# Rotary embedding with interleaved pairs: one buffer of five rows, and neighbouring rows in one transfer

## The chip, the cores and the metric

The kernel runs on one core of one Trainium2 chip. The metric is the device time of one execution in microseconds; shown is the median of three runs with the lowest and the highest.

## The reference

`x` has 8 batch rows of 2048 positions, 16 heads and 64 values in float32 (8.39 MB per row). Neighbouring values of a head are a pair, and each pair is turned by an angle that depends on the position and on the pair's place in the head:

```python
x_pairs = x.reshape(batch, seq_len, num_heads, head_dim // 2, 2)
x1 = x_pairs[..., 0]
x2 = x_pairs[..., 1]
cos = cos[None, :, None, :].copy()
sin = sin[None, :, None, :].copy()
out1 = x1 * cos - x2 * sin
out2 = x1 * sin + x2 * cos
out = np.stack([out1, out2], axis=-1).reshape(batch, seq_len, num_heads, head_dim)
```

Every value is read once from HBM and written once to HBM, both in float32.

## The kernel before

The unit of work is a batch row. Its 2048 positions lie on 128 partitions, 16 neighbouring positions on each (`K = 16`), so a partition holds one run of 64 KB of float32 in HBM and 32 KB of bfloat16 on the chip. The conversion from float32 to bfloat16 and back is done by the transfers themselves, and all these are issued by GpSimd: one queue (q0 in the profile), worked off in the order of issue by 16 DMA engines, each of which carries 8 partitions. Five buffers of one row each hold rows 0 to 4; rows 5, 6 and 7 take the buffers of rows 0, 1 and 2 once these are stored.

`rotate` (L71) turns a row in its buffer, with three VectorE instructions: a product with the sine table into a work buffer (L84), a product with the cosine table in place (L85), and the sum of the two with the work buffer read in swapped pairs (L90). Both tables are made once (L103 to L108), with the signs in the sine table.

The order of the instructions on each engine is the order of the program (`manual_schedule`). The start:

- SyncE loads the first four positions of row 0 as float32 (L94), and ScalarE converts them (L102). This is the other queue, q1.
- GpSimd issues the other twelve positions of row 0 (L95), cosine and sine (L96, L97), rows 1 to 3 (L98, L99), and row 4 in two transfers (L100, `load_fine`): twelve positions, then four positions in packets of at most 8 KB (L63, L64).

Then the loop over rows (L110): rotate a row, issue its store (L69), and from row 1 on issue the load of the row four further on (L122), which waits until the buffer's earlier row has been stored. Store 0 is issued as soon as row 0 is rotated, and so stands in the queue behind all five rows' loads. Between store 0 and store 1 GpSimd copies one element of row 4's last position into `mark` (L117): GpSimd waits there until row 4 has landed, so that store 1 and all that follows is issued after that.

The end: GpSimd stores the first twelve positions of row 7 (L123). The last four go another way: ScalarE writes one element of row 6's buffer (L128), which has to wait until store 6 has landed, then converts the four positions into float32 (L129), and SyncE stores them (L130) beside the twelve.

Of the kernel before, what the change touches and what calls it, by code (L numbers as in the profile page):

```python
# [2 lines left out]

# [4 lines left out]


@with_exitstack  # L10
def kernel(
    ctx: ExitStack,
    tc: tile.TileContext,
    x: bass.AP,
    cos: bass.AP,
    sin: bass.AP,
    out: bass.AP,
):
    nc = tc.nc
    fp32 = mybir.dt.float32  # L20
    bf16 = mybir.dt.bfloat16
    mult = mybir.AluOpType.mult
    add = mybir.AluOpType.add

    B, S, H, D = x.shape
    P = 128
    K = S // P
    KP = 16
    D2 = D // 2
    HD = H * D  # L30
    NX = 5
    HEAD = 4
    TAIL = 4
    FINE = 4
    FINE_BYTES = 8192


    x_t = x.rearrange("b (p k) h d -> b p k (h d)", p=P, k=K)
    out_t = out.rearrange("b (p k) h d -> b p k (h d)", p=P, k=K)
    cos_t = cos.rearrange("(p k) c -> p (k c)", p=P, k=K)  # L40
    sin_t = sin.rearrange("(p k) c -> p (k c)", p=P, k=K)

    consts = ctx.enter_context(tc.tile_pool(name="consts", bufs=1))
    xpool = ctx.enter_context(tc.tile_pool(name="xpool", bufs=NX))
    stage = ctx.enter_context(tc.tile_pool(name="stage", bufs=1))

    cos_sb = consts.tile([P, K * D2], fp32)
    sin_sb = consts.tile([P, K * D2], fp32)
    c_tab = consts.tile([P, K, D], bf16)
    s_tab = consts.tile([P, K, D], bf16)  # L50

    mark = consts.tile([1, 1], bf16)
    tiles = {}

    def load(b, k0=0):
        if b not in tiles:
            tiles[b] = xpool.tile([P, K, HD], bf16, name="xt")
        nc.gpsimd.dma_start(out=tiles[b][:, k0:], in_=x_t[b, :, k0:])  # L58

    def load_fine(b):  # L60
        tiles[b] = xpool.tile([P, K, HD], bf16, name="xt")
        k0 = K - FINE
        nc.gpsimd.dma_start(out=tiles[b][:, :k0], in_=x_t[b, :, :k0])  # L63
        nc.gpsimd.dma_start(  # L64
            out=tiles[b][:, k0:], in_=x_t[b, :, k0:], max_dma_last_dim=FINE_BYTES
        )

    def store(b, k1=K):
        nc.gpsimd.dma_start(out=out_t[b, :, :k1], in_=tiles[b][:, :k1])  # L69

    def rotate(b, k0, k1):  # L71
        nk = k1 - k0
        xp = tiles[b][:, k0:k1]
        qt = stage.tile([P, KP, HD], bf16, name="qt", tag="work")

        def rows(a):
            return a.rearrange("p k (h e) -> p k h e", h=H, e=D)

        def tab(a):
            return dataclasses.replace(  # L80
                a, offset=a.offset + k0 * D, ap=[a.ap[0], [D, nk], [0, H], [1, D]]
            )

        nc.vector.tensor_tensor(out=rows(qt[:, :nk]), in0=rows(xp), in1=tab(s_tab), op=mult)  # L84
        nc.vector.tensor_tensor(out=rows(xp), in0=rows(xp), in1=tab(c_tab), op=mult)  # L85
        q_swap = dataclasses.replace(
            qt, offset=qt.offset + 1, ap=[qt.ap[0], [2, nk * HD // 2], [-1, 2]]
        )
        x3 = xp.rearrange("p k (a j) -> p (k a) j", j=2)
        nc.vector.tensor_tensor(out=x3, in0=x3, in1=q_swap, op=add)  # L90

    with tc.manual_schedule():
        head = stage.tile([P, TAIL, HD], fp32, name="st", tag="work")
        nc.sync.dma_start(out=head[:, :HEAD], in_=x_t[0, :, :HEAD])  # L94
        load(0, HEAD)  # L95
        nc.gpsimd.dma_start(out=cos_sb, in_=cos_t)  # L96
        nc.gpsimd.dma_start(out=sin_sb, in_=sin_t)  # L97
        for b in range(1, NX - 1):  # L98
            load(b)  # L99
        load_fine(NX - 1)  # L100

        nc.scalar.copy(out=tiles[0][:, :HEAD], in_=head[:, :HEAD])  # L102
        s2 = s_tab.rearrange("p k (i j) -> p (k i) j", j=2)  # L103
        nc.vector.tensor_copy(out=s2[:, :, 0], in_=sin_sb)  # L104
        nc.vector.tensor_scalar_mul(s2[:, :, 1], sin_sb, -1.0)  # L105
        nc.vector.tensor_copy(  # L106
            out=c_tab.rearrange("p k (i j) -> p (k i) j", j=2),
            in_=cos_sb.to_broadcast([P, K * D2, 2]),  # L108
        )
        for b in range(B):  # L110
            if b == 0:
                rotate(b, 0, HEAD)
                rotate(b, HEAD, KP)
            else:
                rotate(b, 0, KP)
            if b == 1:
                nc.gpsimd.tensor_copy(out=mark, in_=tiles[NX - 1][:1, K - 1, :1])  # L117
            if b < B - 1:
                store(b)

            if b >= 1 and b - 1 + NX < B:
                load(b - 1 + NX)  # L122
        store(B - 1, K - TAIL)  # L123

        tail = stage.tile([P, TAIL, HD], fp32, name="st", tag="work")
        nc.scalar.copy(out=tiles[B - 2][:1, 0, :1], in_=tiles[B - 1][:1, K - 1, :1])  # L128
        nc.scalar.copy(out=tail, in_=tiles[B - 1][:, K - TAIL :])  # L129
        nc.sync.dma_start(out=out_t[B - 1, :, K - TAIL :], in_=tail)  # L130


# [1 line left out]
_INS = ['x', 'cos', 'sin']  # L134
_OUTS = [((8, 2048, 16, 64), 'float32')]


# [23 lines left out]
```

## Time and profile before

| what | value |
|---|---|
| median of 3 runs (lowest to highest) | 317.47 us (317.16 to 317.57) |
| span of the profiled execution | 315.7 us |
| transfers issued by GpSimd, by SyncE | 19, 2 |
| VectorE idle for want of a row, before rows 5, 6 and 7 | 3.7, 12.4 and 12.6 us |
| last instruction's issue (SyncE's store of row 7's end) | 299.25 us, 15.6 us to landing |

The span is that of one execution under the profiler; what the device time has beyond it lies before the first and after the last instruction. "To landing" is the time from the start of a transfer's issue to the moment when all 16 DMA engines have reported it done; since transfers queue up, it holds the wait behind the earlier ones. The GB/s of a load count its bfloat16 side, half of what is read from HBM.

### The profile page before, as it was taken

How to read it: one execution, taken by the hardware profiler on the slowest of the kernel's cores; microseconds unless marked ns; L12 is line 12 of the kernel's file. 1: busy time of each engine (PE TensorE's matmuls, PEld its weight loads, DVE VectorE, ACT ScalarE, POOL GpSimd, SP SyncE). 2: the span in 40 equal slices, each digit the busy share in tenths (PEclk: the TensorE clock that was granted, in tenths of full speed). 3: DMA queues.
4: the chain of work that ended last, by engine and by line, in shares of the span. 5: the costliest groups of instructions: out<-in, count | busy, mean ns of one | idle time of the engine just before them, and what ended most of it. 6: DMA issues, size and time to landing. Idle time of an engine off the chain costs nothing.

```text
span 315.7 us, 127 instructions
## 1 busy us (share of the span) xinstructions
DVE 210.4 (67%) x30; ACT 8.6 (3%) x4; POOL 12.6 (4%) x24
## 2 busy tenths in 40 slices
DVE  0009999999999999999869960899508994000000
ACT  1030000000000000000000000000000000000400
POOL 6000000000000201010000100000000000000000
DMA  7999999999999999999999999999999999999997
GB/s 257 257 282 199 199 228 237 199 199 257 201 206 266 399 482 448 399 332 257 208 399 399 394 203 199 432 498 266 199 291 440 399 399 515 415 399 423 426 432 313
DMA packets 3025, 102.24 MB, mean 324 GB/s; under 512 B 337, under 2 KB 337, under 8 KB 721
## 3 DMA queue, kind: packets, MB, share of 16 engines
q0 software_dynamic: 2736, 98.04, 96.8%
q1 hardware_dynamic: 288, 4.19, 3.3%
q14 instruction: 1, 0.00, 0.0%
HBM read 67.63 MB, written 67.11 MB: 427 GB/s over the span
## 4 chain that ended last, share of the span: by engine, by line
another core or an unknown queue 88%; DMA 5%; ACT 1%; ACTq 1%; issue 0%
DMA st<-in_x_dram 5%; ACT xt L102 1%; ACTq L156 1%; ACT xt L128 0%; ACTq L128 0%
## 5 line engine op out<-in xcount | busy, mean ns | idle before, releaser
L84 DVE TENSOR_TENSOR qt<-xt,s_tab 128x16384 bf16<-128x16384 bf16 (+2 forms) x9 | 69.7, 7744 | 28.8 <-DMA xt<-in_x_dram 28.6
L85 DVE TENSOR_TENSOR xt<-xt,c_tab 128x16384 bf16<-128x16384 bf16 (+2 forms) x9 | 69.7, 7743 | 0.4
L90 DVE TENSOR_TENSOR xt<-xt,qt 128x16384 bf16<-128x16384 bf16 (+2 forms) x9 | 69.7, 7744 | 0.3
L104 DVE CAST s_tab<-sin_sb 128x512 bf16<-128x512 f32 x1 | 0.5, 453 | 23.9 <-DMA sin_sb<-in_sin_dram 23.9
L69 POOL DMA_DIRECT2D out_dram<-xt x8 | 4.3, 538 | 128.7 <-DVE xt L90 128.7
L128 ACT COPY xt<-xt 1x1 bf16<-1x1 bf16 x1 | 0.2, 192 | 276.6 <-DMA out_dram<-xt 276.6
L58 POOL DMA_DIRECT2D xt<-in_x_dram x7 | 3.9, 572 | 73.8 <-DMA out_dram<-xt 73.0
L102 ACT CAST xt<-st 128x4096 bf16<-128x4096 f32 x1 | 3.6, 3604 | 13.3 <-DMA st<-in_x_dram 13.3
L117 POOL COPY mark<-xt 1x1 bf16<-1x1 bf16 x1 | 2.0, 1965 | 49.3 <-DMA xt<-in_x_dram 49.3
L129 ACT CAST st<-xt 128x4096 f32<-128x4096 bf16 x1 | 3.6, 3598 | 0.0
L102 ACT ACT_TABLE_LOAD x1 | 1.3, 1283 | 0.7 <-PEq L145 0.7
L64 POOL DMA_DIRECT2D xt<-in_x_dram x1 | 0.8, 782 | 0.0
L106 DVE CAST c_tab<-cos_sb 128x1024 bf16<-128x1024 f32 x1 | 0.7, 683 | 0.0
L63 POOL DMA_DIRECT2D xt<-in_x_dram x1 | 0.6, 599 | 0.0
L97 POOL DMA_DIRECT2D sin_sb<-in_sin_dram x1 | 0.6, 562 | 0.0
L96 POOL DMA_DIRECT2D cos_sb<-in_cos_dram x1 | 0.6, 554 | 0.0
L105 DVE TENSOR_SCALAR s_tab<-sin_sb 128x512 bf16<-128x512 f32 x1 | 0.4, 444 | 0.0
L145 POOL MEMSET const-float32-0.0<- 128x1 f32 x1 | 0.1, 98 | 0.2 <-issue 0.2
L145 POOL MEMSET const-bfloat16-1.0<- 128x1 bf16 x1 | 0.1, 101 | 0.0
L145 POOL MEMSET const-float32-1.0<- 128x1 f32 x1 | 0.1, 98 | 0.0
L145 POOL MEMSET const-uint8-127<- 128x1 uint8 x1 | 0.1, 98 | 0.0
## 6 DMA issues: line engine op xcount, KB each, us to landing
xt<-in_x_dram POOLq DMA_DIRECT2D x6, 4096.0 KB, 57.6
xt<-in_x_dram POOLq DMA_DIRECT2D x2, 3072.0 KB, 56.5
out_dram<-xt POOLq DMA_DIRECT2D x1, 6144.0 KB, 47.8
st<-in_x_dram SPq DMA_DIRECT2D x1, 2048.0 KB, 14.6
out_dram<-st SPq DMA_DIRECT2D x1, 2048.0 KB, 15.6
xt<-in_x_dram POOLq DMA_DIRECT2D x1, 1024.0 KB, 97.2
cos_sb<-in_cos_dram POOLq DMA_DIRECT2D x1, 256.0 KB, 21.3
sin_sb<-in_sin_dram POOLq DMA_DIRECT2D x1, 256.0 KB, 21.4
```

The source lines that it names most:

```text
L58: nc.gpsimd.dma_start(out=tiles[b][:, k0:], in_=x_t[b, :, k0:])
L63: nc.gpsimd.dma_start(out=tiles[b][:, :k0], in_=x_t[b, :, :k0])
L64: nc.gpsimd.dma_start(out=tiles[b][:, k0:], in_=x_t[b, :, k0:], max_dma_last_dim=FINE_BYTES)
L69: nc.gpsimd.dma_start(out=out_t[b, :, :k1], in_=tiles[b][:, :k1])
L84: nc.vector.tensor_tensor(out=rows(qt[:, :nk]), in0=rows(xp), in1=tab(s_tab), op=mult)
L85: nc.vector.tensor_tensor(out=rows(xp), in0=rows(xp), in1=tab(c_tab), op=mult)
L90: nc.vector.tensor_tensor(out=x3, in0=x3, in1=q_swap, op=add)
L102: nc.scalar.copy(out=tiles[0][:, :HEAD], in_=head[:, :HEAD])
L106: nc.vector.tensor_copy(out=c_tab.rearrange("p k (i j) -> p (k i) j", j=2), in_=cos_sb.to_broadcast([P, K * D2, 2]),)
L117: nc.gpsimd.tensor_copy(out=mark, in_=tiles[NX - 1][:1, K - 1, :1])
L129: nc.scalar.copy(out=tail, in_=tiles[B - 1][:, K - TAIL :])
L156: with _tile.TileContext(nc) as tc:
```

## The change

The five buffers become one tile of five rows, so that neighbouring rows are neighbours on the chip too, and the views of `x` and `out` have the partition ahead of the batch row. `load` and `store` take a number of rows. Rows 1 and 2 are loaded by one transfer, rows 5 and 6 also; rows 0 and 1, 3 and 4, 5 and 6 are stored by one transfer each. Row 4 is loaded as fourteen positions and two, without a bound on the size of packets. The copy into `mark` on GpSimd goes. In its place `hold` puts two copies of one element on ScalarE: the first reads the last of the fourteen positions, the second writes an element of row 0 onto itself; the store of rows 0 and 1 has to wait for the second, and ScalarE's order puts it behind the first. The tables, the instructions of `rotate`, the first transfer by SyncE and the last one stay as they were.

```diff
-    x_t = x.rearrange("b (p k) h d -> b p k (h d)", p=P, k=K)
-    out_t = out.rearrange("b (p k) h d -> b p k (h d)", p=P, k=K)
+    x_t = x.rearrange("b (p k) h d -> p b k (h d)", p=P, k=K)
+    out_t = out.rearrange("b (p k) h d -> p b k (h d)", p=P, k=K)
...
-    def load_fine(b):
-        tiles[b] = xpool.tile([P, K, HD], bf16, name="xt")
-        k0 = K - FINE
-        nc.gpsimd.dma_start(out=tiles[b][:, :k0], in_=x_t[b, :, :k0])
-        nc.gpsimd.dma_start(
-            out=tiles[b][:, k0:], in_=x_t[b, :, k0:], max_dma_last_dim=FINE_BYTES
-        )
+    buf = rows_pool.tile([P, NX, K, HD], bf16, name="xt")
 
-    def store(b, k1=K):
-        nc.gpsimd.dma_start(out=out_t[b, :, :k1], in_=tiles[b][:, :k1])
+    def place(b, n=1, k0=0, k1=K):
+        return buf[:, b % NX : b % NX + n, k0:k1]
+
+    def load(b, n=1, k0=0, k1=K):
+        nc.gpsimd.dma_start(out=place(b, n, k0, k1), in_=x_t[:, b : b + n, k0:k1])
+
+    def store(b, n=1, k0=0, k1=K):
+        nc.gpsimd.dma_start(out=out_t[:, b : b + n, k0:k1], in_=place(b, n, k0, k1))
...
+    def hold(b, after):
+
+        one = buf[:1, b % NX, 0, :1]
+        nc.scalar.copy(out=mark, in_=after)
+        nc.scalar.copy(out=one, in_=one)
...
-        for b in range(1, NX - 1):
-            load(b)
-        load_fine(NX - 1)
+        load(1, 2)
+        load(3)
+        load(4, k1=K - LAST)
+        load(4, k0=K - LAST)
...
-            if b == 1:
-                nc.gpsimd.tensor_copy(out=mark, in_=tiles[NX - 1][:1, K - 1, :1])
-            if b < B - 1:
-                store(b)
-
-            if b >= 1 and b - 1 + NX < B:
-                load(b - 1 + NX)
-        store(B - 1, K - TAIL)
-
+        rotate(0, 0, HEAD)
+        rotate(0, HEAD, K)
+        rotate(1)
+        hold(0, buf[:1, 4, K - LAST - 1, :1])
+        store(0, 2)
+        rotate(2)
+        store(2)
+        load(5, 2)
+        rotate(3)
+        rotate(4)
+        store(3, 2)
+        load(7)
+        rotate(5)
+        rotate(6)
+        store(5, 2)
+        rotate(7)
+        store(7, k1=K - TAIL)
```

`LAST` is 2. GpSimd issues 14 transfers: row 0's twelve positions, cosine, sine, rows 1 and 2, row 3, row 4 twice, then store 0 and 1, store 2, load 5 and 6, store 3 and 4, load 7, store 5 and 6, and the twelve positions of store 7.

More of the change, by code (lines that the diff above doesn't have):

```diff
@@ L27 @@
     K = S // P
-    KP = 16
     D2 = D // 2
@@ L33 @@
     TAIL = 4
-    FINE = 4
-    FINE_BYTES = 8192
-    x_t = x.rearrange("b (p k) h d -> b p k (h d)", p=P, k=K)
-    out_t = out.rearrange("b (p k) h d -> b p k (h d)", p=P, k=K)
+    LAST = 2
+    x_t = x.rearrange("b (p k) h d -> p b k (h d)", p=P, k=K)
+    out_t = out.rearrange("b (p k) h d -> p b k (h d)", p=P, k=K)
     cos_t = cos.rearrange("(p k) c -> p (k c)", p=P, k=K)
@@ L43 @@
     consts = ctx.enter_context(tc.tile_pool(name="consts", bufs=1))
-    xpool = ctx.enter_context(tc.tile_pool(name="xpool", bufs=NX))
+    rows_pool = ctx.enter_context(tc.tile_pool(name="rows", bufs=1))
     stage = ctx.enter_context(tc.tile_pool(name="stage", bufs=1))
@@ L52, with rotate @@
     mark = consts.tile([1, 1], bf16)
-    tiles = {}
-    def load(b, k0=0):
-        if b not in tiles:
-            tiles[b] = xpool.tile([P, K, HD], bf16, name="xt")
-        nc.gpsimd.dma_start(out=tiles[b][:, k0:], in_=x_t[b, :, k0:])
-    def load_fine(b):
-        tiles[b] = xpool.tile([P, K, HD], bf16, name="xt")
-        k0 = K - FINE
-        nc.gpsimd.dma_start(out=tiles[b][:, :k0], in_=x_t[b, :, :k0])
-        nc.gpsimd.dma_start(
-            out=tiles[b][:, k0:], in_=x_t[b, :, k0:], max_dma_last_dim=FINE_BYTES
-        )
-    def store(b, k1=K):
-        nc.gpsimd.dma_start(out=out_t[b, :, :k1], in_=tiles[b][:, :k1])
-    def rotate(b, k0, k1):
+    buf = rows_pool.tile([P, NX, K, HD], bf16, name="xt")
[5 more added lines that the diff above has]
+        nc.gpsimd.dma_start(out=out_t[:, b : b + n, k0:k1], in_=place(b, n, k0, k1))
+    def rotate(b, k0=0, k1=K):
         nk = k1 - k0
-        xp = tiles[b][:, k0:k1]
-        qt = stage.tile([P, KP, HD], bf16, name="qt", tag="work")
+        xp = buf[:, b % NX, k0:k1]
+        qt = stage.tile([P, K, HD], bf16, name="qt", tag="work")
         def rows(a):
@@ L90, in rotate @@
         nc.vector.tensor_tensor(out=x3, in0=x3, in1=q_swap, op=add)
+    def hold(b, after):
+        one = buf[:1, b % NX, 0, :1]
+        nc.scalar.copy(out=mark, in_=after)
+        nc.scalar.copy(out=one, in_=one)
     with tc.manual_schedule():
         head = stage.tile([P, TAIL, HD], fp32, name="st", tag="work")
-        nc.sync.dma_start(out=head[:, :HEAD], in_=x_t[0, :, :HEAD])
-        load(0, HEAD)
+        nc.sync.dma_start(out=head[:, :HEAD], in_=x_t[:, 0, :HEAD])
+        load(0, k0=HEAD)
         nc.gpsimd.dma_start(out=cos_sb, in_=cos_t)
         nc.gpsimd.dma_start(out=sin_sb, in_=sin_t)
-        for b in range(1, NX - 1):
-            load(b)
-        load_fine(NX - 1)
-        nc.scalar.copy(out=tiles[0][:, :HEAD], in_=head[:, :HEAD])
+        load(1, 2)
+        load(3)
+        load(4, k1=K - LAST)
+        load(4, k0=K - LAST)
+        nc.scalar.copy(out=buf[:, 0, :HEAD], in_=head[:, :HEAD])
         s2 = s_tab.rearrange("p k (i j) -> p (k i) j", j=2)
@@ L109 @@
         )
[L110 to L115, printed above, removed]
-            if b == 1:
-                nc.gpsimd.tensor_copy(out=mark, in_=tiles[NX - 1][:1, K - 1, :1])
-            if b < B - 1:
-                store(b)
-            if b >= 1 and b - 1 + NX < B:
-                load(b - 1 + NX)
-        store(B - 1, K - TAIL)
+        rotate(0, 0, HEAD)
[15 more added lines that the diff above has]
+        store(7, k1=K - TAIL)
         tail = stage.tile([P, TAIL, HD], fp32, name="st", tag="work")
-        nc.scalar.copy(out=tiles[B - 2][:1, 0, :1], in_=tiles[B - 1][:1, K - 1, :1])
-        nc.scalar.copy(out=tail, in_=tiles[B - 1][:, K - TAIL :])
-        nc.sync.dma_start(out=out_t[B - 1, :, K - TAIL :], in_=tail)
+        nc.scalar.copy(out=buf[:1, 1, 0, :1], in_=buf[:1, 2, K - 1, :1])
+        nc.scalar.copy(out=tail, in_=buf[:, 2, K - TAIL :])
+        nc.sync.dma_start(out=out_t[:, 7, K - TAIL :], in_=tail)
 _INS = ['x', 'cos', 'sin']
```

## The prediction

> **What bounds the kernel now.** I began with the page: busy time by engine, the 40 slices, the DMA queues.
>
> ```profile
> DVE 210.4 (67%) x30; ACT 8.6 (3%) x4; POOL 12.6 (4%) x24
> DMA  7999999999999999999999999999999999999997
> q0 software_dynamic: 2736, 98.04, 96.8%
> q1 hardware_dynamic: 288, 4.19, 3.3%
> HBM read 67.63 MB, written 67.11 MB: 427 GB/s over the span
> ```
>
> No compute engine is busy for much over two thirds of the span, but the 16 DMA engines are: 96.8% and 3.3% of their time belong to the GpSimd queue and the SyncE queue, and only the first and the last slice show a 7. The kernel is a conveyor of transfers, almost all in one queue, and its time is the sum of what the queue carries plus every moment in which it carries less. The chain of waits can't follow that queue (it calls 88% "another core or an unknown queue"), so I used the DMA issues in narrow windows: start of the issue (timeline) plus time to landing. That gives landings at 81.7 us (row 3), 96.2 (twelve positions of row 4), 102.3 (its last four), 121.6 (store 0), 140.9 (store 1), 160.2 (load 5), 179.6 (store 2) and 295.5 (store 6). Two lines of this, from the issue view:
>
> ```profile
> xt<-in_x_dram POOLq DMA_DIRECT2D x1, 3072.0 KB, 91.7
> xt<-in_x_dram POOLq DMA_DIRECT2D x1, 1024.0 KB, 97.2
> ```
>
> Issued at 4.54 and 5.06, they landed at 96.2 and 102.3. From 102.25 to 295.46 ten whole rows pass: 19.32 us each, loads and stores alike, back to back. Against this measure one place stands out: the last four positions of row 4 took 102.25 - 96.24 = 6.0 us, where a quarter of 19.32 is 4.83. The windows show when the 1.2 us were lost (columns: length, busy time of DVE, ACT and POOL, PE clock, DMA share, GB/s):
>
> ```profile
> 95.95:98.20 2.25, 2.25 (x1) 0.00 (x0) 0.00 (x0) 1.00 1.06 215
> 98.25:101.00 2.75, 2.75 (x1) 0.00 (x0) 0.00 (x0) 1.00 1.06 147
> ```
>
> The fine load ran at 215 GB/s (bf16 side) and then at 147 GB/s, shortly before the first store's turn. That store had been in the queue since 52.4 us. The transitions from whole-row loads to stores (160.2 to 179.6) lose nothing.
>
> The third view is the first issues, because the change needs the price of a GpSimd transfer that starts into an empty queue:
>
> ```profile
> 0.74 0.38 SPq L94 DMA_DIRECT2D st<-in_x_dram  x1
> 1.24 0.67 POOL L58 DMA_DIRECT2D xt<-in_x_dram  x1 [0.80 <-PEq L156]
> ...
> 5.06 0.78 POOL L64 DMA_DIRECT2D xt<-in_x_dram  x1
> 102.30 1.97 POOL L117 COPY mark<-xt 1x1 bf16<-1x1 bf16 x1 [49.29 <-DMA xt<-in_x_dram]
> ```
>
> SyncE's issue ended at 1.12 and its first packet began at 1.75, 0.63 us later. GpSimd's ended at 1.91, yet up to 5.5 us the DMA view has packets of q1 only; q0's first began at 5.51, 3.6 us later. In between the engines worked off SyncE's packets of about 0.62 us, and a queue that comes in late is served only behind what is already taken up: at the end SyncE's store, issued at 299.25, got its first packet at 305.4, behind some three packets of 1.81 us. Three of 0.62 leave 3.6 - 1.9 = 1.7 us.
>
> **The change, part by part.** All against the profiled execution: span 315.69 us, and 1.78 us around it to the median of 317.47.
>
> *Fewer transfers.* GpSimd issues 14 instead of 19; five joins vanish. A row's eight packets per engine are 2.41 us apart, 19.28 together, so a join costs 19.32 - 19.28 = 0.04 us at most; bounds 0 and 0.2 for five, and I take **-0.15 us**. Issues on GpSimd (0.53 to 0.78 us each) lie beside the transfers and save nothing.
>
> *Rows 1 and 2 land together.* Row 1 can't be rotated when it landed before, but only at 62.4 with row 2: its rotation starts 10.5 us later than at 51.9. A rotation is 3 x 8.73 = 26.2 us. Rows 1 and 2 are done at 114.8, and store 2 is wanted in the queue at about 140; rows 3 and 4 at 167, wanted at 198. Rows 5 and 6 land together at 198 and are done at 250.4, wanted when load 7 ends, 256: 5.5 us of cover, the thinnest (before: store 4 issued at 225.3, wanted at 237.5). The issue and even 3.6 us after it fit. Cost **0**. The tail keeps its form: row 6's store must land, then a cast of 3.6 us, then SyncE's store under the twelve positions of store 7. Cost 0.
>
> *The old mark on GpSimd (1.97 us) goes.* It lay beside store 0. Nothing.
>
> *Row 4 in 14 + 2 with the hold.* Fourteen positions land at 81.73 + 14/16 x 19.32 = 98.63; the two need 2.41 and would end at 101.05. Before, the same point of the queue was reached at 102.25. So **-1.2 us**, if the slow stretch goes: only half as many small packets, and no store behind them while they run. If it stays in full, 0.
>
> *The wait against it.* The store of rows 0 and 1 is issued only after 98.63. ScalarE starts 0.02 after a landing (its cast at 15.32 after 15.30); its two copies take 0.09 to the next start and 0.19, so 0.28; GpSimd starts 0.29 after its release (store 5 at 186.77, after DVE's 186.47); the issue, for two rows, is priced by the one that also writes two packets per partition, 0.78. It ends at 98.63 + 0.02 + 0.28 + 0.29 + 0.78 = 100.0. Then the unseen term: 0.63 us (SyncE's) to 3.6 us (GpSimd's first, uncorrected). To compare with landings I add 0.34, the lag of a landing behind its last packet (count written at 101.90, landing 102.24). Landing clock at which the store may begin: 100.97 to 103.94. At the lower end there is no gap; at the upper one it is 2.9 us. The nearest row is GpSimd's own, 1.7 after correction, but it is the first of a program and its correction is rough; I take halfway to SyncE's, 1.15: start at 101.5, gap **+0.45 us**. Behind the waiting store on GpSimd stand store 2 (its data come at 114.8) and load 5, and behind the copies on ScalarE only the tail: nobody else is late.
>
> The Trainium skill's page "DMA: Bandwidth & Descriptors", section "Specifications", gives about 1 us to the first byte on the GpSimd path; counted from the issue's start this would leave no gap, and the estimate by it is 317.47 - 1.2 - 0.15 = 316.1. The trace does not bear it out at the one place it could: 5.51 - 1.24 = 4.3 us there, other packets ahead included.
>
> Sum: -0.15 - 1.2 + 0.45 = -0.9; and 0.1 to 0.2 for filling the engines anew (SyncE's first packets took 0.73 to 1.5 instead of 0.62): **-0.75 us, 316.7**.
>
> **Rivals.** (1) *Even*: the start takes the 1.7 us of GpSimd's first row; gap 1.0; 317.47 - 1.2 - 0.15 + 1.0 + 0.15 = 317.3. The same comes out where the slow stretch belongs to the switch and not to the small packets: then the hold wins nothing and loses little. Within 0.2% of 317.47 (0.63 us, about what a measurement here can tell from none) lie 316.84 to 318.10. (2) *Slower, a dry queue*: the full 3.6 us; gap 2.9; 317.47 - 1.2 - 0.15 + 2.9 = 319.0. It decides from about 2.6 us after the issue on. For it: the only start of that queue in the trace; against it: packets ahead of it. (3) *Slower, locked out*: at 102.30 GpSimd's one-element copy took 1.97 us and ended at 104.27, just when DVE's instruction ended (104.23). If writing the store's packets were held so, then at 99.2 row 2's second product is running, from 62.4 + 4 x 8.73 = 97.3 to 106.1: start at about 107, 4.8 us later than before, 322.1. Against it: issues at 121.9 and 141.2 took 0.53 us with DVE at work. The Trainium skill's "SBUF — State Buffer", section "Who interferes with whom", holds that a product of two SBUF tensors blocks a GpSimd instruction that reads SBUF, and not one that only writes; by that rule the copy's wait is explained and rival 3 falls. (4) *Slower, the pairs*: packets of two rows cost more, or the 5.5 us of cover at store 5 is used up; 0.04 us on each of an engine's 16 packets of a pair would be 3.2 us in five pairs, and 316.7 + 3.2 = 319.9. No row shows it.
>
> **How the numbers follow.** Forecast 0.46 (faster); rival 1 0.27 (same); rival 2 0.18, rival 3 0.04, rival 4 0.05 (slower, 0.27). The range runs from no gap and every gain (317.47 - 1.2 - 0.2 = 316.1, down to 316.0 for the rounding) to rival 2's 319.0. The forecast's own range is 316.0 to 316.8.
>
> **What would show it.** After: the 14 positions land near 98.6; the two about 2.4 us later; the store's issue starts near 99.2 and takes 0.6 to 0.8; landings of pairs 38.6 us apart; a stretch without packets of at most 0.5 us near 101. A longer one is rival 1 or 2, one to 106 rival 3; the two still landing 3 us or more after the 14 says that the slow stretch stays; pairs over 38.7 us, or an idle DMA near 256, rival 4. I am wrong if the store starts after 102.3.

## The result, and the profile after

| | before | after |
|---|---|---|
| median (lowest to highest) | 317.27 us (316.99 to 317.57, 6 runs) | 316.31 us (316.20 to 316.67, 6 runs) |
| span of the profiled execution | 315.7 us | 314.9 us |
| row 3 landed | 81.73 | 81.79 |
| row 4 whole on the chip | 102.25 | 101.58 |
| row 6 stored | 295.46 | 294.70 |

The ratio is 0.9971, 95% interval 0.9960 to 0.9982: about 1 us faster. The prediction counted from 317.47 us, the median of the three runs it had; beside the changed kernel, six runs of the kernel before gave 317.27. The profiled execution was the slowest of its six (316.67 us), so its span shows 0.8 of the 0.96 us between the medians.

The times in the table are issue plus time to landing, as before. They say where the 0.8 us of the two profiles came from: 0.73 of it lies between the landings of rows 3 and 4 (20.52 us before, 19.79 after). From row 4's landing to row 6's store it is 193.12 instead of 193.21 us, and from there to the last landing 19.35 instead of 19.36.

The issues of row 4 in the changed kernel (queue, size, time to landing; they were issued at 4.27 and 4.79 us):

```profile
xt<-in_x_dram POOLq DMA_DIRECT2D x1, 3584.0 KB, 94.8
xt<-in_x_dram POOLq DMA_DIRECT2D x1, 512.0 KB, 96.8
```

Fourteen positions landed at 99.04, 17.26 us after row 3, where 14/16 of 19.32, 16.91, is the measure; so this execution lost some 0.35 us before the last two positions. These landed at 101.58, 2.5 us later where 2.41 is the measure. The timeline around it:

```profile
97.36 8.69 DVE L76 TENSOR_TENSOR xt<-xt,c_tab 128x16384 bf16<-128x16384 bf16 x1
99.07 0.19 ACT L86 COPY mark<-xt 1x1 bf16<-1x1 bf16 x1 [80.20 <-DMA xt<-in_x_dram]
99.16 0.19 ACT L87 COPY xt<-xt 1x1 bf16<-1x1 bf16 x1
99.64 0.72 POOL L60 DMA_DIRECT2D out_dram<-xt  x1 [94.27 <-ACT xt L87]
```

ScalarE's two copies, then GpSimd's issue of the first store, which ends at 100.36. What the DMA engines carried meanwhile, in three stretches (length, DVE, ACT, POOL, PE clock, DMA share, GB/s):

```profile
98.70:100.50 1.80, 1.80 (x1) 0.29 (x2) 0.72 (x1) 1.00 1.06 214
```

```profile
100.36:100.92 0.56, 0.56 (x1) 0.00 (x0) 0.00 (x1) 1.00 0.92 183
100.92:101.30 0.38, 0.38 (x1) 0.00 (x0) 0.00 (x0) 1.00 6.43 2760
```

The two positions ran at 214 GB/s; the stretch at 147 is gone. The last small packets begin by 100.9, and at 100.93 the store's first packets begin (bytes count at a packet's start, hence the 2760). The queue did not run dry: the store came when the load was through, within a tenth of a microsecond.

### The profile page after: what moved, and what is told of

The parts are those of the page before. It is cut to its first block, busy times and chain, and to the rows that moved or that the text cites. A ratio compares the mean times of both kernels' runs of the same rounds, so it can differ in the third digit from the quotient of the medians.

```text
span 314.9 us, 117 instructions
## 1 busy us (share of the span) xinstructions
DVE 210.4 (67%) x30; ACT 8.9 (3%) x6; POOL 8.9 (3%) x18
## 4 chain that ended last, share of the span: by engine, by line
DVE 58%; DMA 14%; another core or an unknown queue 13%; ACTq 1%; issue 0%; ACT 0%; DVEq 0%
DVE xt L76 19%; DVE xt L81 19%; DVE qt L75 19%; DMA out_dram<-xt 14%; ACTq L157 1%; DVE c_tab L104 0%; ACT xt L129 0%; DVEq L75 0%; ACTq L129 0%; DVEq L76 0%
## 5 line engine op out<-in xcount | busy, mean ns | idle before, releaser
L60 POOL DMA_DIRECT2D out_dram<-xt x5 | 3.3, 657 | 248.1 <-DVE xt L81 153.8
L57 POOL DMA_DIRECT2D xt<-in_x_dram x7 | 4.3, 638 | 26.0 <-DMA out_dram<-xt 25.2
```

What stands on the lines that cost most here:

```text
L57: nc.gpsimd.dma_start(out=place(b, n, k0, k1), in_=x_t[:, b : b + n, k0:k1])
L60: nc.gpsimd.dma_start(out=out_t[:, b : b + n, k0:k1], in_=place(b, n, k0, k1))
```

## The experiments

Twelve kernels. Each ratio is to the kernel before, measured beside it (its medians were 317.30 to 317.39 us). "Loss" is the time from the landing of the transfer ahead to that of the last load before the first store, less 19.32 us per row; each comes from one profile, and landings scatter by up to some 0.4 us where no store stands behind them (the fourteen positions took 17.26 us in the changed kernel and 16.95 in e5). "After sine" counts from the landing of the sine table, the transfer ahead of row 1. Where a difference to the changed kernel (316.31) is small, it compares runs that were not taken side by side.

**e1: the hold taken away.**

```diff
-        hold(0, buf[:1, 4, K - LAST - 1, :1])
         store(0, 2)
```

> The changed kernel without the hold: the store of rows 0 and 1 is issued when row 1 is rotated (near 89 us) and stands in the queue behind row 4's fourteen and two positions. Theory A (the slow stretch needs small packets with a store queued behind them; the hold keeps the store away until they are through): the slow stretch is back, the two positions land 3.0 us or more after the fourteen instead of 2.54, and the median is 316.6 to 317.1, that is 0.3 to 0.8 us above the changed kernel's 316.31. Theory B (the gain comes from having 8 small packets per DMA engine instead of 16): the two land 2.5 us after the fourteen and the median stays at 316.3.

Median 317.30 us, ratio to the kernel before 0.9998 (0.9989 to 1.0007). The two positions landed 3.5 us after the fourteen, the loss is 20.47 - 19.32 = 1.15 us:

```profile
97.90:98.30 0.40, 0.40 (x1) 0.00 (x0) 0.00 (x0) 1.00 1.06 205
98.30:100.80 2.50, 2.50 (x1) 0.00 (x0) 0.00 (x0) 1.00 1.02 138
```

With eight small packets per engine and the store in the queue the slow stretch is back, 138 GB/s. The median is 1.0 us above the changed kernel's, more than the 0.3 to 0.8 that theory A gave, and nothing of the gain is left: it hangs on the hold. Theory B falls.

**e2: no small packets either.** As e1, and row 4 is one transfer.

```diff
-        load(4, k1=K - LAST)
-        load(4, k0=K - LAST)
+        load(4)
...
-        hold(0, buf[:1, 4, K - LAST - 1, :1])
```

> The changed kernel with row 4 loaded whole in one transfer and no hold, the first store queued behind it. Theory A: no small packets, so no slow stretch; row 4 lands 19.3 us after row 3 and the pair of stores 38.6 us later; median about 315.8, below the changed kernel's 316.31. Rival C (the loss belongs to the first switch from loads to stores, whatever the size of packets): row 4 and the first pair together take 0.6 to 1.2 us more than 57.9, median 316.4 to 317.0.

Median 317.27, ratio 0.9998 (0.9989 to 1.0006); loss 20.66 - 19.32 = 1.34 us, and each engine's last packet of row 4 took 3.2 to 3.5 us in the trace where the others took 2.43 to 2.53. Theory A was wrong about the small packets: they only make visible what a large packet suffers too. Rival C held, with more than its 0.6 to 1.2 us.

**e4: a dry start.** Row 4 whole, and the hold on its last position.

```diff
-        load(4, k1=K - LAST)
-        load(4, k0=K - LAST)
+        load(4)
...
-        hold(0, buf[:1, 4, K - LAST - 1, :1])
+        hold(0, buf[:1, 4, K - 1, :1])
```

> The changed kernel with row 4 loaded whole and the hold put on its last position: nothing is in the queue while the first store is issued. This is the price of a dry start. From the changed kernel's trace (14 positions landed 99.04, issue 99.64 to 100.36, first packet 100.93) it is 0.3 of landing lag + 0.6 + 0.72 + at most 0.57, so 1.9 to 2.2 us without a packet, and the median 317.5 to 318.2. If a GpSimd transfer into an empty queue needs 3.6 us after its issue (rival 2 of the prediction) the stretch is 5.2 us and the median near 321.

Median 318.46, ratio 1.0037 (1.0025 to 1.0050), a little over the range expected.

```profile
101.45 0.19 ACT L86 COPY mark<-xt 1x1 bf16<-1x1 bf16 x1 [82.59 <-DMA xt<-in_x_dram]
101.55 0.19 ACT L87 COPY xt<-xt 1x1 bf16<-1x1 bf16 x1
102.03 0.72 POOL L60 DMA_DIRECT2D out_dram<-xt  x1 [97.18 <-ACT xt L87]
```

```profile
101.15:103.30 2.15, 2.15 (x1) 0.28 (x2) 0.72 (x1) 1.00 0.00 0
103.30:103.50 0.20, 0.20 (x1) 0.00 (x0) 0.00 (x0) 1.00 12.16 5243
```

A load's "count" is the small packet in which an engine reports its share done. The queue was dry from the last count at 101.13 to the first packet at 103.32: 2.2 us, of which 0.57 lie behind the issue. A held-back GpSimd transfer into an empty queue costs that much, and not the 5.2 us that it would with the 3.6 behind the issue of the prediction's second rival. The packets that follow are normal (2.43 us): the 1 us of e1 and e2 is not hidden in the dry start, it does not occur.

**e5: no pairs.** One transfer per row again, with 14 + 2 and the hold.

```diff
-        load(1, 2)
+        load(1)
+        load(2)
...
-        store(0, 2)
+        store(0)
+        store(1)
```

(and so with rows 3 to 6; the loads go back to the places that they had in the kernel before)

> The changed kernel with every pair taken apart again into one transfer per row, loads and stores in the order of the kernel before; row 4 in 14 and 2 and the hold stay, now on store 0. Theory A: the joins are worth 0.1 to 0.2 us, so the median is 316.4 to 316.5, still 0.8 below the kernel before. Rival D (the pairs bring the gain, by fewer transfers): 317.0 or more.

Median 316.42, ratio 0.9980 (0.9969 to 0.9990); loss 19.44 - 19.32 = 0.12 us. Rival D falls: the gain does not need the pairs. What they add, 0.1 us by the medians, is not clear of the noise. Of the eight executions, two took 317.30 and 317.31 us, as long as e1 and e2, and the other six 316.27 to 316.61; no profile of the two long ones was kept, and their cause is open.

**e7: one position of cover.** `LAST = 1`.

> The changed kernel with LAST = 1: fifteen positions, the hold, one position as cover (1.2 us instead of 2.4). The chain from the fifteen's landing to the first packet of the store is at most 1.9 us plus 0.3 of landing lag. e4, without cover, had 2.3 us between the last count and the first packet, so the gap here should be 2.3 - 1.2 = 1.1 us, the median 316.3 + 1.1 = 317.4. If the hold needs less cover than that (the issue overlapping the last packets in some other way), 316.3.

Median 317.40, ratio 1.0001 (0.9991 to 1.0010).

```profile
100.52 0.72 POOL L60 DMA_DIRECT2D out_dram<-xt  x1 [95.15 <-ACT xt L87]
```

```profile
100.90:101.80 0.90, 0.90 (x1) 0.00 (x0) 0.34 (x1) 1.00 0.00 0
101.80:102.00 0.20, 0.20 (x1) 0.00 (x0) 0.00 (x0) 1.00 12.16 5243
```

Near the 1.1 us expected: a gap of 0.9 us, first packet at 101.81, again 0.57 after the issue's end at 101.24.

**e3: four positions of cover.** `LAST = 4`.

> The changed kernel with LAST = 4: the store is issued about 1.3 to 1.9 us after the twelve positions' landing, with 4.8 us of load still to come, so it stands in the queue some 3 us before the four positions end. Theory A2: the slow stretch is back in their last packets, the four land 5.8 to 6.0 us after the twelve, median 317.2. If only a store queued long before (tens of us) costs it: 4.9 us, 316.3.

Median 317.00, ratio 0.9992 (0.9982 to 1.0001). The store's issue ended at 97.56; the four positions landed 5.6 us after the twelve, the loss is 0.8 us. The windows:

```profile
96.20:98.10 1.90, 1.87 (x2) 0.28 (x2) 0.72 (x1) 1.00 1.03 216
98.10:100.40 2.30, 2.30 (x1) 0.00 (x0) 0.00 (x0) 1.00 1.08 167
100.40:101.00 0.60, 0.60 (x1) 0.00 (x0) 0.00 (x0) 1.00 0.98 205
```

The slow packets begin at 98.1, 2.9 us before the store's first packet at 101.0, and the last packet of each engine takes 0.62 us again, as before 98.1. That is also 0.6 us after the issue's end, so e3 doesn't tell whether the store's arrival in the queue or the nearness of its turn sets their start. A store that is ready some 3 us before its turn is enough to cost most of the gain. Of the three covers tried, two positions is the one at which the store comes neither early nor late.

**e8: the mark of the kernel before taken away**, so that store 1 too is queued early.

```diff
-            if b == 1:
-                nc.gpsimd.tensor_copy(out=mark, in_=tiles[NX - 1][:1, K - 1, :1])
```

> The kernel before without the copy into mark: store 1 is issued when row 1 is rotated, near 78 us, and not at 104; store 0 is queued since 52 us as before. Theory A2 (what costs is that a store, one or many, is in the queue when the last load's packets end): unchanged, 317.2 to 317.5. If the amount of stores queued behind matters: slower, 318 or more.

Median 317.26, ratio 0.9998 (0.9989 to 1.0008), loss 0.88 us. The loss stays with two stores queued as with one. Here too the last packets run at the normal rate again: 212 GB/s from 96.0 to 98.2 us, 152 to 100.0, then 193 up to 101.0.

**e6: an early store.** The question left was why later switches from loads to stores cost nothing.

```diff
         load(1, 2)
-        load(3)
-        load(4, k1=K - LAST)
-        load(4, k0=K - LAST)
...
         rotate(0, 0, HEAD)
+        store(0, k1=HEAD)
+        load(3)
+        load(4)
         rotate(0, HEAD, K)
         rotate(1)
-        hold(0, buf[:1, 4, K - LAST - 1, :1])
-        store(0, 2)
+        store(0, k0=HEAD)
+        store(1)
```

> The queue switches from loads to stores once more, earlier: the first four positions of row 0 are stored between the load of rows 1 and 2 and the load of row 3; row 4 is loaded whole, no hold, rows 0 and 1 are stored in two further transfers. e2 lost about 1 us in the last packets of row 4, before its first store. Theory F (the first store of the program costs it, once): the loss of about 1 us stands at the early store, near 62 us (rows 1 and 2 and the four positions together take 44.4 us from 23.7 instead of 43.4), and rows 3 and 4 with store 0's twelve positions pass at 19.3 us per row; median 317.3 or a little more. Theory H (a load that ends while VectorE works, with a store queued behind it, is slowed): both switches lose 1 us, median 318.3. Theory G (a long stretch of loads alone before the switch costs it, five rows but not two): the loss is at 62 or at neither place, and not near 106.

Median 317.42, ratio 1.0002 (0.9992 to 1.0012). Rows 1 and 2 landed at 63.54, 39.68 us after sine: loss 1.04 us, before the early store. Rows 3 and 4 then took 38.65 us for two rows, no loss before the next store. VectorE was idle at the first place, from 51.9 us on until row 1 landed, and working at the second: theory H falls.

**e9 and e10: a small store at the very start**, issued ahead of all of GpSimd's loads, from ScalarE's queue (e9, the lines below) or GpSimd's (e10); otherwise e2.

```diff
+        nc.vector.memset(blank, 0.0)
+        nc.scalar.dma_start(out=out_t[:, 7, K - 1, :256], in_=blank)
```

> e2 (row 4 whole, no hold, the first pair of stores queued behind it, 317.27) with one small store added at the very start, when the DMA engines are idle: VectorE writes zeros into 1 KB on each of the 128 partitions, ScalarE's own queue stores them into a corner of the output that the last store writes over. Theory F (the first store that a DMA engine carries costs it 1 us, once, whatever the queue): the loss at the end of row 4 (20.66 us from row 3's landing instead of 19.3) is gone or down to a few tenths, row 4 lands 19.3 us after row 3, median 316.2 to 316.5, with up to 0.5 us for the small store itself at the start. Theory Q (the first store of the GpSimd queue costs it): unchanged at the end of row 4, median 317.3 to 317.7.

> The same small store, issued by GpSimd as its first transfer (bfloat16 zeros, converted by the transfer as all its stores are), so it is the first store of that queue. Theory F and theory Q both expect the loss at the end of row 4 to be gone: row 4 lands 19.3 us after row 3, median 316.2 to 316.8 (GpSimd's loads are issued 0.6 us later, but SyncE's load keeps the engines busy until then). If the loss stays (20.6 us), it is neither the engine's nor the queue's first store, and theory S remains: it is paid at the first switch from a long run of loads to a long run of stores, or by the first store whose data lie in the buffers.

Medians 317.43 and 317.28, ratios 1.0004 (0.9994 to 1.0013) and 0.9998 (0.9988 to 1.0007). The loss at the end of row 4 was 0.83 and 0.62 us, against 1.34 in e2: smaller, but not gone. The engines' last packets of row 4 took 3.0 to 3.4 and 2.9 to 3.3 us, where the ones ahead took 2.43. The medians don't show the difference, since the small store cost about as much at the start (sine landed at 24.28 and 24.30 us, against 23.67 in e2). The test was also less clean than meant: the engines were not idle, since SyncE's load had been moving since 1.74 us, and the small store's packets began only at 5.5 us, among packets of loads. Theories F and Q as they were put fall: a store of 1 KB packets, the first of the engines or of the queue, takes away a part of the loss at most.

**e11: the early store one row earlier**, behind row 1 instead of rows 1 and 2.

Against e6:

```diff
-        load(1, 2)
+        load(1)
...
         store(0, k1=HEAD)
+        load(2)
         load(3)
```

> e6 with the early store of row 0's first four positions one row earlier in the queue: behind row 1, near 43 us, instead of behind rows 1 and 2, near 63; after it rows 2, 3 and 4 are loaded one by one (58 us of loads alone) and then row 0's other twelve positions stored. In e6 the loss stood at the early store, after 60 us of loads, and not at the second switch, after 39 us of loads. Theory G (a switch to stores costs about 1 us after a long run of loads, 58 us or more, and nothing after 39 us): no loss near 43 us (a run of 41 us), a loss of about 1 us near 106; median 317.3. Theory F2 (the first store of any size worth the name costs it, once, wherever it stands): row 1 lands 20.3 us after sine instead of 19.3, and no loss near 106; median 317.3. No loss at either place would make the kernel 316.2 to 316.4, without a hold.

Median 317.57, ratio 1.0007 (0.9998 to 1.0017). Row 1 landed 20.71 us after sine, a loss of 1.39 us; rows 2, 3 and 4 took 57.94 us for 57.96. So the length of the run of loads is not it (G falls), and the first store behind loads pays. The windows around row 1's last packets:

```profile
37.00:39.70 2.70, 2.67 (x2) 0.00 (x0) 0.00 (x0) 1.00 0.90 194
39.70:43.50 3.80, 3.80 (x1) 0.00 (x0) 0.00 (x0) 1.00 1.00 138
```

**e12: the early store cut to one position.** Against e11:

```diff
-        store(0, k1=HEAD)
+        store(0, k1=1)
...
-        store(0, k0=HEAD)
+        store(0, k0=1)
```

> e11 with the early store cut to row 0's first position (0.5 MB, packets of 4 KB; the other fifteen positions go where the twelve went). e11 paid about 1.3 us at the end of row 1, just ahead of its early store of four positions, and nothing near 106; the small store of zeros at the very start (e9, e10; packets of 1 KB) did not spare the loss near 100. Theory F2 (the first store issued behind loads costs 1.0 to 1.3 us once, whatever its size): row 1 lands 20.3 to 20.7 us after sine, no loss near 106, median 317.3 to 317.6. Theory F3 (a store must be of some size to count): little loss near 43 (row 1 lands 19.3 to 19.6 us after sine), and about 1 us at the end of row 4; median again 317.3. A small loss at 43 and none near 106 would be a median of 316.3 to 316.8 without a hold.

Median 316.56, ratio 0.9977 (0.9967 to 0.9986). The same windows:

```profile
37.00:39.70 2.70, 2.67 (x2) 0.00 (x0) 0.00 (x0) 1.00 0.90 194
39.70:42.40 2.70, 2.70 (x1) 0.00 (x0) 0.00 (x0) 1.00 0.98 194
```

Row 1 landed 19.48 us after sine, a loss of 0.16 us, within the scatter; the engines' last packets of row 1 took 2.5 to 2.8 us, against 3.4 to 4.0 in e11. Rows 2 to 4 took 57.95 us, no loss, and the store of fifteen positions behind them 18.15 for 18.11. The case that the expectation named last came out: without a hold, and without the pairs of rows 0 to 2, a store of 0.5 MB behind the first row cures the loss as well. The median is not below that of the changed kernel and the intervals overlap, so it is not a better version, only a second cure.

## Why the prediction was right

The forecast was 316.7 us, faster; 316.31 was measured. As a change it is -0.75 forecast and -0.96 measured. Step by step:

- *The bound.* Right: the time follows the landings in one queue, and nearly all of the difference (0.73 of the two profiles' 0.79 us) is found between two of them.
- *Fewer transfers, -0.15 us.* Not contradicted, and too small to confirm: 0.1 us between e5 and the changed kernel's medians, and 0.09 in the landings from row 4 to row 6's store, both within the scatter.
- *Rows 1 and 2 together, 0.* Right: row 1's rotation began at 62.45, store 2 was issued at 115.07, and store 5, the thinnest place, at 250.81 against load 7's landing at 256.05: 5.2 us of cover instead of 5.5.
- *Row 4 in 14 + 2, -1.2 us if the slow stretch goes.* It went, and the gain was 0.73 us in this profile, which lost some 0.35 before the last two positions, and 1.08 in e5's. Of the two reasons given beside it, "only half as many small packets" was wrong (e1 has as many and lost 1.15, e2 has none and lost 1.34); "no store behind them while they run" was right. The step had the size about right and half of the cause.
- *The gap, +0.45 us.* Mis-sized: it was nothing. The chain up to the issue's end was as counted (the fourteen's landing, then 0.03, 0.28, 0.29 and 0.72 against 0.02, 0.28, 0.29 and 0.78); the landing itself was 0.4 later than 98.63, which leaves the cover as it was, since the two end later too. The unseen term, taken as 1.15, was 0.57 in the changed kernel, e4 and e7 alike, close to the lower bound from SyncE's row (0.63). GpSimd's own first row (3.6, corrected to 1.7) was the wrong neighbour. What held it up at the start of the program was not tried.
- *Filling the engines anew, +0.1 to 0.2.* Nothing: the store's first packets took 2.43 us.

That the sum came so close is in part luck. The two costs that were not there (0.45 and 0.15) stood against a gain that came out smaller than forecast: without them the sum would have been -1.35, further from the -0.96 measured than the -0.75 was.

The Trainium skill's page "DMA: Bandwidth & Descriptors", section "Specifications", has about 1 us to the first byte on this path. Counted from the start of the issue, the changed kernel, e4 and e7 have 1.29 us, 0.72 of it the issue; so the page was nearer than the prediction's own choice (0.78 and 1.15).

The rivals. (1) *Even*: its second half said that the hold wins nothing where the slow stretch belongs to the switch and not to the small packets. e2 shows that the small packets are not needed for it, and the changed kernel against e1 that the hold still wins everything: a store that isn't in the queue doesn't slow the load. That inference was the weakest sentence of the prediction. (2) *A dry queue*: even without any cover (e4) the queue was dry for 2.2 us, and 0.57 of it, not 3.6, lay behind the issue. (3) *Locked out*: the issue at 99.64 fell into VectorE's product (97.36 to 106.05) and its packets began at 100.93. This agrees with the rule of the Trainium skill's "SBUF — State Buffer", section "Who interferes with whom", that such a product does not block a GpSimd instruction that only writes. (4) *The pairs*: four of the five took 38.55 to 38.65 us, as two rows. The store of rows 3 and 4 took 38.96, over the 38.7 that the prediction named as a sign of this rival, but the load behind it then took 19.02; the three rows together are 57.98 us for 57.96, so nothing was lost.

## What to carry to other kernels

A queue that looks full can still lose time at one place: lay the landings side by side, each against the measure of its size, and the place shows itself. A wait ahead of an issue can be worth more than an early issue, if the transfer that it delays would disturb the one in flight; then just enough of the transfer in flight has to be left to cover the wait. One position was too little (`LAST = 1`: a gap of 0.9 us) and four too much (`LAST = 4`: 0.8 us lost again). To price a transfer into an empty queue, make the queue empty in an experiment rather than take the program's first transfer.

## What the runs showed of the hardware

- The first large store that stands behind loads in the queue slows packets of the load ahead of it, which costs 0.8 to 1.4 us in e1, e2, e3, e6, e8, e11 and the kernel before. Where the packets are small enough to show it (e1, e3, e8 and the kernel before), the slow ones begin 2.7 to 2.9 us before the store's first packet, and the load's very last ones run at the normal rate again. Later switches from loads to stores cost nothing, after 39 us (e6) or 58 us (e11) of loads.
- It is not paid by a store that comes when the loads are through (the changed kernel, e4, e7), and hardly by a small one: 0.16 us for packets of 4 KB (e12), after which the next store finds nothing to pay. A store of 1 KB packets at the start of the program took away a part of the loss at most (0.83 and 0.62 us were left in e9 and e10). What inside the DMA engines is being paid for remains open; that the early store's size, and not only its place, decides between 1.39 and 0.16 us rests on one pair of runs, e11 and e12.
- From the end of a GpSimd issue to the first packet in an empty queue it is 0.57 us (e4, e7; in the changed kernel, whose queue had just run through, the same); from the last count of a load over landing, hold and issue to that packet 2.2 us.
